# Gathers kept out of the first three retrievals, embedding products in other PSUM banks, two first-stage blocks run earlier

## The chip, the cores and the metric

The kernel runs on one core of one Trainium2 chip. The metric is the device time of one execution in microseconds (us). Five engines run side by side, each in the order of its own instruction list: TensorE (PE, matmuls; PEld is its weight loads), VectorE (DVE), ScalarE (ACT), GpSimd (POOL, which issues the indirect gathers) and SyncE (SP, which issues the other transfers).

## What is computed

One layer of a decoder for 512 prompt tokens and 64 sample tokens (576 in all), model width 1024. First comes a projection with window attention and a gated unit, and their merge. Then a layer of experts, PEER: every token scores 2 x 128 keys for each of 8 heads, takes the best 16 of the 16 x 16 pairs of a head ("retrieval"), and uses those 16 of 16384 one-neuron experts. Last comes a gated embedding.

```python
    def one_block(xb):
        q = (xb @ w_q).reshape(blk, PEER_HEADS, 2, PEER_HALF)
        sc = jnp.einsum('thcd,hcnd->thcn', q, sub_keys).astype(jnp.float32)
        s_top, i_top = lax.top_k(sc, PEER_TOPK)
        ...
        best, pos = lax.top_k(cand, PEER_TOPK)
        idx = jnp.take_along_axis(cand_idx, pos, axis=-1)
        gate = jax.nn.softmax(best, axis=-1)
        u = expert_u[idx]
        act = jax.nn.gelu(jnp.einsum('thkd,td->thk', u, xb).astype(jnp.float32))
        w = (gate * act).astype(xb.dtype)
        return jnp.einsum('thk,thkd->td', w, expert_v[idx])
...
    x2 = x1 + _peer(_rms_norm(x1, lp['ffn_norm_g']), ...)
    gate = jax.nn.sigmoid(_rms_norm(x2, lp['ple_norm_g']) @ lp['w_ple_gate'])
    x3 = x2 + gate * (p_i @ lp['w_ple'])
```

## The kernel before

Tokens lie in five tiles: the 64 sample tokens and four of 128. The experts of the first two tiles (192 tokens) are *gathered*: for every token and each of 128 slots a row of `peer_u`, and later one of `peer_v`, comes by an indirect transfer (L720, 512 KB each). A gather of `peer_u` ends in one DVE instruction that multiplies and sums (L732), one of `peer_v` in one that scales and adds (L739). That makes 192 + 192 = 384 gathers. The other three tiles (384 tokens) go through *all* experts as dense matmuls: stage 1 multiplies the tokens with each of 128 blocks of `peer_u`, GELU follows, the result is multiplied with a gate matrix G that is zero but at the retrieved experts, and stage 2 multiplies it with `peer_v`.

In float32 a product is made of three matmuls of halves: `split` writes the high half of a weight block on ACT (`w_hi`, L69) and the rest on DVE (`w_lo`, L70). The weight tiles have three or four buffers.

The program after the projections, in the order in which it is written:

- *Retrievals* `retrieve(0)` to `retrieve(2)`, nearly all DVE work: candidates (L624 to L629), the best 16 (L637 to L641), and lookups by comparison and sum (L682, L658, L660, L666, L699), with copies on ACT between (L645, L692). They are written as generators; at each of their steps one first-stage block `stage1()` is placed (24 matmuls at L85, GELU at L789, in turn into the PSUM banks `pv` and `mm`), until `S1_TOPK[ti]` blocks stand in all. At some steps a tile of the embedding product `ple()` (L828, 12 matmuls of 512 columns, emptied by ACT at L830) and of a transpose of rows (`x1_rows()`, L842) follows.
- *Gate phase*: 24 steps `tb`. `build_g` makes the one-hot operands `oa` and `ob` (L862, L865, L868 on DVE, L859 and L860 on ACT) and multiplies them on PE into the banks `sc` and `pt` (L876), which ACT empties (L882). `make_ew` (L798) turns what a retrieval found. First-stage blocks are placed until a goal per step is reached, and the last two retrievals (`retrieve(3)`, `retrieve(4)`) run in the first 7 steps.
- *Stage 2*: 128 steps `j`, each 18 matmuls (L1013), with the remaining first-stage blocks in its first 86 steps or so.

Gathers are placed by credits: `pay(x)` adds x and places as many gathers as the credit holds. `GP` is the credit per first-stage block in the three phases, `GT` the credit per step of the gate phase (its first 7 steps, and the rest), `G2` the credit per step of stage 2 (with and without a first-stage block in it). Before `retrieve(0)` is through there is nothing to gather.

A list scheduler puts the instructions of each engine in order, by the order in which they are written, by their dependencies, by raised priorities (`tc.high_priority`) and by costs of its own. Each engine then runs its list in that order.

```python
    def pay(x):
        credit[0] += x
        n = int(credit[0])
        credit[0] -= n
        gather(n, mark_pe[0])
...
        ps = (mm() if j % 2 or phase[0] > 1 else bank("pv"))[:, :NB]
```

Of the kernel before, what the change touches and what calls it, by code (L numbers as in the profile page):

```python
# [23 lines left out]
NJ = 128  # L24
TB = 16
JB = 8
GP = [0.5, 0.0, 1.65]
G2 = (1.6, 2.0)
SPILL = set(range(2, 40, 2))
NSP = len(SPILL)  # L30
GT = (2.0, 3.5)
ONE = (1, 2)
TAIL0 = 112
TAIL1 = 122
S1_TOPK = (4, 9, 13)
TBK = 7
S1_END = 6
RUN = 2
# [12 lines left out]
def tile_decoder_step(ctx: ExitStack, tc: tile.TileContext, a, o):  # L51
# [16 lines left out]
    def split(src, hi, lo):  # L68
        A.activation(hi, src, AF.Copy)  # L69
        V.tensor_sub(lo, src, hi.bitcast(F32))  # L70
# [59 lines left out]
    def bank(tag):  # L130
        return psB.tile([P, 512], F32, name=tag)
# [47 lines left out]
    with tc.high_priority(offset=500):  # L179
        for cols in HALVES:  # L180
            ps = bank("sc")[:, :cols.stop - cols.start]
# [63 lines left out]
    for g in range(4):  # L245
# [7 lines left out]
        if g == 0:  # L253
            pv = bank("pt")
# [3 lines left out]
            pv = bank("pt")  # L258
# [279 lines left out]
    for c0, r in tilesA:  # L538
# [4 lines left out]
        for hh in range(2):  # L543
            hs = slice(hh * 512, (hh + 1) * 512)
            pt = bank("pt")
# [180 lines left out]
    def gather_steps():  # L726
        for ti, ns in ((0, NS), (1, P)):
            dots = gp.tile([P, P], F32, name="dots")
            wts = gp.tile([P, P], F32, name="wts")
            for s in range(ns):  # L730
                row_ = gather_row(a["peer_u"], ixs[ti][:, s:s + 1])
                V.scalar_tensor_tensor(row_, row_, 1.0, xrs[ti], op0=ALU.mult, op1=ALU.mult,  # L732
                                       accum_out=dots[:, s:s + 1])
                yield
            A.activation(wts[:, :ns], dots[:, :ns], AF.Gelu_apprx_tanh)
            V.tensor_tensor(wts[:, :ns], wts[:, :ns], gts[ti][:, :ns], op=ALU.mult)
            for s in range(ns):
                row_ = gather_row(a["peer_v"], ixs[ti][:, s:s + 1])
                V.scalar_tensor_tensor(accs[ti], row_, wts[:, s:s + 1], accs[ti], op0=ALU.mult, op1=ALU.add)  # L739
                yield  # L740
# [22 lines left out]
# [5 lines that stand above are left out]
# [7 lines left out]
    def stage1():  # L775
        nonlocal j1, nlive
        j = j1
        j1 += 1
        w = load_block(a["peer_uT"][j])
        ps = (mm() if j % 2 or phase[0] > 1 else bank("pv"))[:, :NB]  # L780
        tform(ps, w, xb)
        if j in SPILL:
            act = held_x[-1][:, sorted(SPILL).index(j) % 6, :]
        else:
            n = nlive % RING
            nlive += 1
            act = held_x[n // 6][:, n % 6, :] if n < NXP - 6 else (
                acp[0][:, n - NXP + 6, :] if n < RING - 6 else held_x[-1][:, n - RING + 6, :])
        A.activation(act, ps, AF.Gelu_apprx_tanh)  # L789
        acts[j] = act  # L790
        if j in SPILL:
            S.dma_start(ad[sorted(SPILL).index(j)], act)
        pay(GP[phase[0]])

    def make_ew(e0, e1_, gtf):
        pt = bank("pt")
        for q, src in enumerate((e1_, gtf, e0)):
            T.transpose(out=pt[:, q * P:(q + 1) * P], in_=src, identity=ident)  # L798
        ew = ep.tile([P, 4, P], F32, name="ew")
        A.activation(ew[:, 1:4, :], pt[:, 0:3 * P].rearrange("p (a b) -> p a b", a=3), AF.Copy)  # L800
        A.activation(ew[:, 0, :], pt[:, P:2 * P], AF.Copy, scale=-1.0)
        ewT.append(ew)
# [7 lines left out]
    def ple():  # L810
        ws_ = []
        for k in range(2):
            raw = wp.tile([P, D], F32, name="w_raw", bufs=4)
            S.dma_start(raw, a["w_ple"][k])
            ws_.append([plp.tile([P, D], F32R, name=nm) for nm in ("wph", "wpl")])
            split(raw, *ws_[k])
        for c0, r in TILES:
            pt = plp.tile([P, 2, P], F32, name="pt")
            S.dma_start(pt[:, :, :r], a["pT"][:, :, c0:c0 + r])
            ph, pl = (plp.tile([P, 2, P], F32R, name=nm) for nm in ("ph", "pl"))  # L820
            split(pt[:, :, :r], ph[:, :, :r], pl[:, :, :r])
            for hh in range(2):
                st = plp.tile([P, 512], F32, name="st")
                ps = bank("pv")
                hs_ = slice(hh * 512, (hh + 1) * 512)
                for k in range(2):
                    for i, (xi, wi) in enumerate(((ph, 0), (ph, 1), (pl, 0))):
                        T.matmul(ps[:r], lhsT=xi[:, k, :r], rhs=ws_[k][wi][:, hs_],  # L828
                                 start=k == 0 and i == 0, stop=k == 1 and i == 2)
                A.activation(st[:r], ps[:r], AF.Copy)  # L830
                S.dma_start(pld[c0:c0 + r, hs_], st[:r])
            yield
# [14 lines left out]
    def build_g(tb):  # L847
# [38 lines left out]
        S.dma_start(gd[:, :, tb].rearrange("c p j t -> p c (j t)"), gs.rearrange("p (c j) t -> p c (j t)", j=JB))  # L886

    ples, xrs_ = ple(), x1_rows()
    for ti in range(3):
        for _ in retrieve(ti, ti < 2):  # L890
            if len(acts) < S1_TOPK[ti]:
                stage1()
# [3 lines left out]
        if ti == 0:  # L896
            steps.append(gather_steps())
        while len(acts) < S1_TOPK[ti]:
            stage1()
# [10 lines left out]
    for tb in range(NB // TB):  # L910
# [9 lines left out]
        if tb < TBK:  # L920
            goal = S1_TOPK[2] + (tb + 1) * (S1_PRE - S1_TOPK[2]) // TBK
        else:
# [6 lines left out]
        for _ in range(2):  # L929
            if rest_t and next(rest_t[0], 1) == 1:  # L930
                rest_t.pop(0)
                make_ew(*found[4 - len(rest_t)])
        pay(GT[tb >= TBK] if tb < 22 else 0)
    while nlive < RING - 1:
# [82 lines left out]
    for j in range(NJ):  # L1017
# [4 lines left out]
        if j and j - 1 not in SPILL and j1 < NJ:  # L1022
            stage1()
        pay(G2[0] if j1 < NJ else G2[1])
        if j == TAIL0:
# [185 lines left out]
```

## Time and profile before

| | us |
|---|---|
| median of 3 runs | 1736.32 (1732.24 to 1738.2) |
| profiled execution | 1734.34 |
| its span, first to last instruction | 1732.6 |
| first retrieval begins / first gate product / first matmul of stage 2 | 484.6 / 571.25 / 857.75 |

In the rows below, a line of the timeline gives start, duration, engine, line of the kernel, operation, output<-inputs, shapes, count, and in brackets how long the engine had stood idle before it and what ended that. Operations on DVE and matmuls on PE overlap a little at their ends, so the time that one takes is read from the start of the next. A line of stretches gives the stretch, its length, and the busy time and count for PE, PEld, DVE, ACT and POOL, then the granted PE clock (1.00 throughout), the share of DMA and GB/s.

### The profile page before, as it was taken

Reading aid. Unit: us, or ns where it says so; the run is one execution under the profiler, and the core shown is the slowest. Engines: PE = TensorE matmul, PEld = TensorE weight load, DVE = VectorE, ACT = ScalarE, POOL = GpSimd, SP = SyncE. Lnnn points to the kernel's source line nnn. Section 1 sums busy time; section 2 is a strip of 40 time slices with the busy share of each in tenths; the row PEclk is TensorE's granted clock in tenths of the full one; section 3 lists DMA queues with packets and bytes.
Section 4 is the critical chain, followed back from the end, with each engine's and each line's share of the span. In section 5 each row is a group of like instructions: output and inputs, shape, how many; then the busy total and the mean of one; then the engine's idle time right before and its main releaser. Section 6 shows DMA issues by size and latency. Waiting matters only on the chain.

```text
span 1732.6 us, 27657 instructions
## 1 busy us (share of the span) xinstructions
PE 1705.1 (98%) x10040; PEld 1554.4 (90%) x10040; DVE 1435.4 (83%) x2880; ACT 859.7 (50%) x1519; POOL 531.3 (31%) x390
## 2 busy tenths in 40 slices
PE   8999999999998999999999999999999999999998
PEld 7988999999988999999988888899988999888877
DVE  7365566579899999999698899998888988999873
ACT  6566442343366999899633333333333433333352
POOL 0000000000011122454255554555544544566400
PEclk9999999999999999999999999999999999999999
DMA  7211232432267778999899999999999999999842
GB/s 239 93 61 50 77 104 93 153 108 97 80 203 253 222 242 266 388 363 369 313 370 353 372 395 397 402 398 382 382 343 349 363 343 324 337 373 383 316 164 79
DMA packets 179481, 459.13 MB, mean 265 GB/s; under 512 B 15504, under 2 KB 78992, under 8 KB 177296
## 3 DMA queue, kind: packets, MB, share of 16 engines
q1 hardware_dynamic: 123760, 255.29, 41.8%
q0 software_dynamic: 55584, 202.07, 31.2%
q8 instruction: 79, 1.29, 0.3%
q14 instruction: 58, 0.48, 0.1%
HBM read 420.67 MB, written 37.36 MB: 264 GB/s over the span
## 4 chain that ended last, share of the span: by engine, by line
PE 77%; DVE 9%; DMA 7%; issue 4%; ACT 2%; POOL 1%; SPq 0%; DVEq 0%; POOLq 0%; ACTq 0%
PE mm L85 35%; PE oacc L1013 24%; PE pv L85 5%; PE pt L876 2%; DMA row<-peer_u,idx 2%; PE oacc L974 2%; PE sc L876 2%; DVE w_lo L70 2%; PE sc L85 1%; POOL row L720 1%; DMA row<-peer_v,idx 1%; DMA x1c<-ad 1%; PE mm L974 1%; DVE row L732 1%; DVE acc L739 1%
## 5 line engine op out<-in xcount | busy, mean ns | idle before, releaser
L69 ACT ACTIVATE w_hi<-w_raw 128x1024 fp32r<-128x1024 f32 x321 | 340.2, 1060 | 365.0 <-PE mm L85 267.4
L720 POOL DMA_INDIRECT row<-peer_u,idx x192 | 262.1, 1365 | 820.4 <-PE pv L85 467.5
L70 DVE TENSOR_TENSOR w_lo<-w_raw,w_hi 128x1024 fp32r<-128x1024 f32 x321 | 391.4, 1219 | 66.7 <-ACT w_hi L69 66.1
L85 PE MATMUL mm<-xd,w_hi 128*128 128x384 f32 x1552 | 400.1, 338 | 0.0
L720 POOL DMA_INDIRECT row<-peer_v,idx x192 | 267.8, 1395 | 237.9 <-DVE acc L739 213.8
L85 PE MATMUL mm<-x,w_hi 128*128 128x320 f32 (+1 forms) x1504 | 305.3, 297 | 0.5 <-ACT qp L749 0.5
L85 PEld LDWEIGHTS mm<-xd,w_hi 128*128 128x128 f32 x1552 | 280.3, 188 | 6.2
L85 PE MATMUL mm<-xd,w_lo 128*128 128x384 f32 x776 | 262.0, 338 | 0.0
L739 DVE SCALAR_TENSOR_TENSOR acc<-row,wts,acc 128x1024 f32<-128x1024 f32 x192 | 245.6, 1279 | 5.1 <-DMA row<-peer_v,idx 4.8
L85 PEld LDWEIGHTS mm<-x,w_hi 128*128 128x128 f32 x1504 | 239.6, 188 | 8.7 <-issue 6.5
L732 DVE SCALAR_TENSOR_TENSOR row<-row,xr 128x1024 f32<-128x1024 f32 x192 | 231.7, 1218 | 14.3 <-DMA row<-peer_u,idx 14.2
L1013 PE MATMUL oacc<-w_hi,wh 128*128 128x512 f32 x768 | 241.5, 395 | 1.2 <-ACT wh L69 1.2
L1013 PE MATMUL oacc<-w_hi,wl 128*128 128x512 f32 x768 | 241.6, 396 | 0.9 <-DVE wl L70 0.9
L1013 PE MATMUL oacc<-w_lo,wh 128*128 128x512 f32 x768 | 241.5, 396 | 0.3 <-DVE w_lo L70 0.3
L85 PE MATMUL mm<-x,w_lo 128*128 128x320 f32 (+1 forms) x752 | 221.2, 294 | 0.0
L1013 PEld LDWEIGHTS oacc<-w_hi,wl 128*128 128x128 f32 x768 | 144.2, 188 | 36.3 <-DVE wl L70 1.6
L1013 PEld LDWEIGHTS oacc<-w_lo,wh 128*128 128x128 f32 x768 | 144.3, 188 | 35.0 <-DVE w_lo L70 0.7
L1013 PEld LDWEIGHTS oacc<-w_hi,wh 128*128 128x128 f32 x768 | 143.6, 188 | 30.2 <-ACT wh L69 1.5
L85 PEld LDWEIGHTS mm<-xd,w_lo 128*128 128x128 f32 x776 | 146.2, 188 | 0.1
L85 PEld LDWEIGHTS mm<-x,w_lo 128*128 128x128 f32 x752 | 141.1, 188 | 1.0 <-issue 0.8
L85 PE MATMUL pv<-xd,w_hi 128*128 128x384 f32 x496 | 131.3, 341 | 0.0
L69 ACT ACTIVATE wh<-x 128x384 fp32r<-128x384 f32 x66 | 34.7, 526 | 164.6 <-PE oacc L1013 160.9
(332 smaller groups left out, 2311.6 us busy)
## 6 DMA issues: line engine op xcount, KB each, us to landing
w_raw<-peer_uT SPq DMA_DIRECT2D x128, 512.0 KB, 6.5
w_raw<-peer_v SPq DMA_DIRECT2D x128, 512.0 KB, 6.8
gd<-gs SPq DMA_DIRECT2D x24, 1024.0 KB, 7.9
gs<-gd SPq DMA_DIRECT2D x15, 1536.0 KB, 9.8
w_raw<-w_in SPq DMA_DIRECT2D x30, 512.0 KB, 3.4
w_raw<-peer_wq SPq DMA_DIRECT2D x16, 512.0 KB, 3.5
w_raw<-w_br SPq DMA_DIRECT2D x8, 512.0 KB, 3.2
w_raw<-w_out SPq DMA_DIRECT2D x8, 512.0 KB, 3.3
```

The costliest lines, as they stand in the source:

```text
L69: A.activation(hi, src, AF.Copy)
L70: V.tensor_sub(lo, src, hi.bitcast(F32))
L85: mark_pe[0] = T.matmul(ps, lhsT=w[wi][:, wk + k, :], rhs=x[xi][k], start=i == 0, stop=i == n - 1)
L720: ins = G.indirect_dma_start(out=row_, out_offset=None, in_=table, in_offset=bass.IndirectOffsetOnAxis(ap=ix, axis=0))
L732: V.scalar_tensor_tensor(row_, row_, 1.0, xrs[ti], op0=ALU.mult, op1=ALU.mult, accum_out=dots[:, s:s + 1])
L739: V.scalar_tensor_tensor(accs[ti], row_, wts[:, s:s + 1], accs[ti], op0=ALU.mult, op1=ALU.add)
L876: ins = T.matmul(pt[:, t * P:(t + 1) * P], lhsT=oa[:, t, :], rhs=ob[:, t, :], start=True, stop=True)
L974: T.matmul(p[:r, :hs.stop - hs.start], lhsT=xi[:, k, :r], rhs=w[k][wi][:, hs], start=k == 0 and xi is xh and wi == 0, stop=k == KC - 1 and ...
L1013: mark_pe[0] = T.matmul(oacc[t][hh], lhsT=wi[:, ts], rhs=vi[:, hh * 512:(hh + 1) * 512], start=j == 0 and last == 0 and vi is vh, stop=j = ...
```

## The change

Four numbers and one name change. No credit is paid for blocks among the retrievals, less in the first 7 steps of the gate phase, and a little more in stage 2. Ten and fifteen instead of nine and thirteen blocks stand at the end of the second and third retrieval; the goals of the gate phase stay, so its first 7 steps place 18 blocks and not 20. The embedding products go to the banks `sc` and `pt` in turn.

```diff
-GP = [0.5, 0.0, 1.65]
-G2 = (1.6, 2.0)
+GP = [0.0, 0.0, 1.65]
+G2 = (1.66, 2.06)
...
-GT = (2.0, 3.5)
+GT = (1.5, 3.5)
...
-S1_TOPK = (4, 9, 13)
+S1_TOPK = (4, 10, 15)
...
             for hh in range(2):
                 st = plp.tile([P, 512], F32, name="st")
-                ps = bank("pv")
+                ps = bank(("sc", "pt")[hh])
```

By the credits, 4 gathers stood before the gate phase and 71 before stage 2, and now 0 and 63; the last one stands in step 119 of stage 2 both times.

What the scheduler makes of it shows at three places. The first is PE at the first embedding tile (the 64 sample tokens, L828) after the fifth first-stage block. Before:

```order
L85 MATMUL pv<-xd,w_lo 128x384
L828 MATMUL pv<-wph,ph 64x512
L828 MATMUL pv<-wpl,ph 64x512
L828 MATMUL pv<-wph,pl 64x512
L828 MATMUL pv<-wph,ph 64x512
L828 MATMUL pv<-wpl,ph 64x512
L828 MATMUL pv<-wph,pl 64x512
L85 MATMUL mm<-xd,w_hi 128x384 x2
```

Now, at the same place:

```order
L85 MATMUL pv<-xd,w_lo 128x384
L828 MATMUL sc<-wph,ph 64x512
L828 MATMUL sc<-wpl,ph 64x512
L828 MATMUL sc<-wph,pl 64x512
L828 MATMUL sc<-wph,ph 64x512
L828 MATMUL sc<-wpl,ph 64x512
L828 MATMUL sc<-wph,pl 64x512
L828 MATMUL pt<-wph,ph 64x512
L828 MATMUL pt<-wpl,ph 64x512
L828 MATMUL pt<-wph,pl 64x512
L828 MATMUL pt<-wph,ph 64x512
L828 MATMUL pt<-wpl,ph 64x512
```

Before, the second half of the tile stood in the middle of the next block; now both halves stand together, in two tags of banks that no block uses.

The second place is PE at the first gate product (L876). Before, after 402 first-stage matmuls:

```order
L85 MATMUL pv<-xd,w_hi 128x384 x2
L85 MATMUL pv<-xd,w_lo 128x384
L876 MATMUL pt<-ob,oa 128x128
L876 MATMUL sc<-ob,oa 128x128 x4
L876 MATMUL pt<-ob,oa 128x128 x3
```

Now, after 430:

```order
L85 MATMUL mm<-xd,w_lo 128x384
L85 MATMUL mm<-xd,w_hi 128x384
L876 MATMUL pt<-ob,oa 128x128 x2
L876 MATMUL sc<-ob,oa 128x128 x4
L876 MATMUL pt<-ob,oa 128x128 x2
```

The first product has moved behind 28 more first-stage matmuls.

The third place is DVE ahead of the operands of that product (`ob` by L862 and L868, `oa` by L865). Before:

```order
L639 MAX best<-c_6706 128x8
L680 TENSOR_TENSOR d_6734<-ib 128x8x15
L641 MAX_INDEX pos<-best,c_6706 128x8
L732 SCALAR_TENSOR_TENSOR row,dots<-row,xr 128x1024
L638 MATCH_REPLACE c_6712<-best,cand 128x50
L862 TENSOR_TENSOR ob<-c_iota,ew 128x512
L868 TENSOR_SCALAR ob<-c_iota,ew 128x128 x2
L70 TENSOR_TENSOR w_lo<-w_raw,w_hi 128x1024
L865 TENSOR_TENSOR oa<-c_iota,ew 128x512
```

Now:

```order
L658 TENSOR_TENSOR pr<-ge,cst 128x2048
L694 TENSOR_REDUCE den<-gate 128x8
L666 TENSOR_TENSOR l_6792<-pr 128x1024
L70 TENSOR_TENSOR w_lo<-w_raw,w_hi 128x1024
L666 TENSOR_TENSOR l_6794<-l_6792 128x512
L660 TENSOR_TENSOR pr<-ge,d_6784 128x2048
L666 TENSOR_TENSOR l_6796<-l_6794 128x256
L666 TENSOR_TENSOR l_6939<-pr 128x1024
L70 TENSOR_TENSOR w_lo<-w_raw,w_hi 128x1024
L862 TENSOR_TENSOR ob<-c_iota,ew 128x512
L865 TENSOR_TENSOR oa<-c_iota,ew 128x512
L868 TENSOR_SCALAR ob<-c_iota,ew 128x128 x4
```

No gather stands there any more, and lookups of the fourth retrieval (L658, L660, L666), which stood behind the first products, now stand ahead of them.

## Prediction

> **What bounds the kernel now.** I read the page's busy times first, then busy times by stretch, then the rows of TensorE (PE) that carry a wait, then the rows of VectorE (DVE) around one point.
>
> ```profile
> PE 1705.1 (98%) x10040; PEld 1554.4 (90%) x10040; DVE 1435.4 (83%) x2880; ACT 859.7 (50%) x1519; POOL 531.3 (31%) x390
> ...
> core 0: us, PE busy (x) PEld busy (x) DVE busy (x) ACT busy (x) POOL busy (x), PEclk, DMA share, GB/s
> 490.00:570.00 80.00, 71.25 (x394) 65.67 (x393) 77.29 (x307) 49.93 (x71) 13.16 (x10) 1.00 0.76 249
> ...
> 700.00:840.00 140.00, 140.00 (x950) 136.25 (x949) 137.76 (x271) 128.65 (x308) 65.12 (x46) 1.00 1.04 369
> ...
> 1050.00:1100.00 50.00, 48.86 (x232) 41.92 (x231) 46.11 (x75) 16.81 (x23) 24.30 (x19) 1.00 1.03 413
> ...
> 1500.00:1600.00 100.00, 100.00 (x430) 80.58 (x429) 97.29 (x96) 36.70 (x48) 68.27 (x48) 1.00 0.99 371
> ```
>
> PE has work 98% of the span, and the change takes no matmul away. So it can gain only time in which PE waits, and lose by making new waits. While the first three retrievals run (490 to 570 us) PE stands idle for 80.00 - 71.25 = 8.75 us while DVE is busy 77.29 of 80 us; in the gate phase proper (700 to 840) both are full. These are the PE waits from 490 us to the end of the gate phase (a small one of 0.16 us left out):
>
> ```profile
> 501.06 0.44 PE L828 MATMUL pv<-wph,ph 128*64 128x512 f32 x1 [2.22 <-ACT x L789]
> 524.68 0.50 PE L828 MATMUL pv<-wph,ph 128*128 128x512 f32 x1 [2.80 <-ACT x L789]
> 552.32 0.50 PE L828 MATMUL pv<-wph,ph 128*128 128x512 f32 x1 [2.64 <-ACT x L789]
> 566.64 0.30 PE L798 MATMUL pt<-c_ident,e 128*128 128x128 f32 x1 [0.92 <-DVE best L639]
> 584.73 1.13 PE L876 MATMUL pt<-ob,oa 128*128 128x128 f32 x8 [0.38 <-DVE oa L865]
> 619.30 0.46 PE L876 MATMUL pt<-ob,oa 128*128 128x128 f32 x2 [0.49 <-DVE best L639]
> 631.58 0.77 PE L876 MATMUL pt<-ob,oa 128*128 128x128 f32 x4 [0.50 <-DVE best L639]
> 696.01 0.68 PE L876 MATMUL pt<-ob,oa 128*128 128x128 f32 x4 [1.22 <-DVE ob L868]
> ```
>
> The embedding products (L828) wait three times, 2.22 + 2.80 + 2.64 = 7.66 us, for ScalarE (ACT) to empty a bank `pv` that a first-stage block (L85) filled; that GELU (L789) comes late behind a table load, as at 521.52 us:
>
> ```profile
> 521.52 1.28 ACT L789 ACT_TABLE_LOAD   x1
> 522.82 0.49 ACT L789 ACTIVATE x<-mm 128x384 f32<-128x384 f32 x1
> ...
> 524.15 0.48 ACT L789 ACTIVATE x<-pv 128x384 f32<-128x384 f32 x1
> ```
>
> The other waits are for DVE, 0.92 + 0.38 + 0.49 + 0.50 + 1.22 = 3.51 us. All together it is 11.2 us, and that is the most that this part of the program can give.
>
> **The change, part by part.**
>
> *Other banks.* `sc` and `pt` are not written by first-stage blocks, so the three waits for L789 go: up to -7.66 us on PE. The new banks are emptied by ACT too (L830). But with two buffers a bank of `sc` comes up again only after two tiles, and one of `pt`, which the row transposes (L842) also use, after one, and between two tiles stand two blocks, 8.3 us by the rows below. The nearest row is the wait of 2.80 us: a bank emptied that late would still be free in time. I take 0 for new waits there and keep 0 to 7.66 as bounds (the upper end is a rival).
>
> *Two blocks moved.* A block is 24 matmuls and takes 4.16 us, by the starts of two that follow each other:
>
> ```profile
> 478.40 0.51 PE L85 MATMUL mm<-xd,w_hi 128*128 128x384 f32 x2
> ...
> 482.56 0.51 PE L85 MATMUL pv<-xd,w_hi 128*128 128x384 f32 x2
> ...
> 571.25 0.46 PE L876 MATMUL pt<-ob,oa 128*128 128x128 f32 x2
> ```
>
> The work is the same wherever it stands; what counts is when PE arrives at the first gate product (571.25 us) and whether DVE has its operands then. By the order of the instructions PE has issued 402 first-stage matmuls ahead of that product before, and 430 now: 28 more, 28/24 x 4.16 = 4.85 us. Without the L828 waits and the 0.92 PE would be there at 571.25 + 4.85 - 7.66 - 0.92 = 567.5 us. Each moved block also issues a 512 KB load on SP's queue earlier, and one of them a store of its activations; the DMA share there is 0.76, against 1.04 in the gate phase, so I cost these at 0. Behind them on SP stand the embedding's stores, which nobody reads before the tail, and the loads of the row transposes, which have a block's time to land. ACT gets two more splits, with 50 us of 80 in use.
>
> *Gathers.* The credits give 4 gathers less by the end of the retrievals (4 to 0) and 4 less in the first seven steps of the gate phase (0.5 x 7, rounded by the credits): 63 instead of 71 when stage 2 begins. Each is one DVE instruction of 1.14 us; 8 are 9.1 us off DVE ahead of stage 2. POOL issues fewer, and is not near its limit (13 of 80 us).
>
> *What DVE does instead.* This is the step that I weigh most. The rows are those of DVE from the third retrieval's comparison (L682) on, and the last operand of the first product (L865):
>
> ```profile
> 546.15 0.64 DVE L637 MAX8 best<-cand 128x8 f32<-128x50 f32 x5
> 546.71 1.21 DVE L682 TENSOR_TENSOR ge<-sp,cst 128x2048 bf16<-128x2048 bf16 x1
> 547.83 1.22 DVE L70 TENSOR_TENSOR w_lo<-w_raw,w_hi 128x1024 fp32r<-128x1024 f32 x1
> 548.97 1.22 DVE L658 TENSOR_TENSOR pr<-ge,cst 128x2048 bf16<-128x2048 bf16 x1
> 550.10 1.22 DVE L732 SCALAR_TENSOR_TENSOR row<-row,xr 128x1024 f32<-128x1024 f32 x1
> ...
> 551.24 1.22 DVE L70 TENSOR_TENSOR w_lo<-w_raw,w_hi 128x1024 fp32r<-128x1024 f32 x1
> 552.38 0.68 DVE L666 TENSOR_TENSOR l<-pr 128x1024 bf16<-128x1024 bf16 x1
> 552.98 0.28 DVE L694 TENSOR_REDUCE den<-gate 128x8 f32<-128x128 f32 x1
> ...
> 570.42 0.69 DVE L865 TENSOR_TENSOR oa<-c_iota,ew 128x512 f32<-128x512 f32 x1
> ```
>
> By the starts, a split, a comparison and a gather take 1.13 to 1.14 us each, the L666 0.60. From L682 to the end of that L865 (571.1 us) it is 24.4 us, and DVE is idle nowhere in it: it comes just in time for PE at 571.25. In the new order the stretch between the same two marks has two gathers less (-2.3) and one split more (+1.1), and the work of the *fourth and fifth* retrieval now stands in it, which stood behind the first products: three operations of 128x2048 (3 x 1.13 = 3.4), four L666 (0.60 + 0.60, and two smaller ones that I estimate at 0.5 together, by their half and quarter width), and 27 small ones. Five of these take 0.56 us here (546.15 to 546.71), so 27 take at least 3.0; others have a preloading row too, and I take 3.9. The sum is -2.3 + 1.1 + 3.4 + 1.7 + 3.9 = +7.8 us: 32.2 us.
>
> The stretch starts earlier by the three gathers ahead of it (3 x 1.14 = 3.4 us), and perhaps by a part of these waits, of which the first goes with its gather:
>
> ```profile
> 513.16 1.23 DVE L732 SCALAR_TENSOR_TENSOR row<-row,xr 128x1024 f32<-128x1024 f32 x1 [0.65 <-DMA row<-peer_u,idx]
> ...
> 530.53 1.23 DVE L699 TENSOR_TENSOR ge<-sp,cst 128x2048 bf16<-128x2048 bf16 x1 [1.36 <-ACT sp L645]
> ```
>
> So the operands of the first product come at 546.71 - 3.4 - 0.65 + 32.2 = 574.9 us, where PE wants them at 567.5. PE waits some 7.4 us there (or for the splits of the blocks shortly ahead, which comes to the same): the wait for the bank has become a wait for DVE. Against before PE is then 571.25 + 4.85 - 574.9 = 1.2 us ahead. Bounds: 2.6 ahead if the 1.36 goes as well, 1.0 behind if the small operations cost 0.2 us each (+1.5) and no DVE wait goes (+0.65).
>
> Behind the first product DVE has that much retrieval work done and four gathers less, so that PE is the slower one. Of the four waits that are left there (0.38 + 0.49 + 0.50 + 1.22 = 2.59) I take half as gone: -1.3, with bounds of -2.6 and +2.
>
> *Stage 2.* Eight gathers more, through 1.66 and 2.06 per step. DVE is at 97.29 of 100 us late in the program, in this pattern of one step:
>
> ```profile
> 1548.37 0.56 DVE L70 TENSOR_TENSOR wl<-aL,wh 128x384 fp32r<-128x384 f32 x1
> 1548.85 1.28 DVE L739 SCALAR_TENSOR_TENSOR acc<-row,wts,acc 128x1024 f32<-128x1024 f32 x1
> 1550.05 1.22 DVE L70 TENSOR_TENSOR w_lo<-w_raw,w_hi 128x1024 fp32r<-128x1024 f32 x1
> ...
> 1552.57 0.56 DVE L70 TENSOR_TENSOR wl<-x,wh 128x384 fp32r<-128x384 f32 x1
> ```
>
> A step lasts 4.20 us; DVE works 0.48 + 1.14 + 2 x 1.20 = 4.02. With 0.06 x 1.20 it is 4.09, still inside, so this costs nothing as long as one late gather (1.20 us, made good in seven steps) is covered by the two buffers of `wl`. About 1090 us, where DMA moves 413 GB/s, PE has lost time already (0.88 us in this row, and 0.26 ahead of it):
>
> ```profile
> 1092.99 0.73 PE L1013 MATMUL oacc<-w_hi,wl 128*128 128x512 f32 x2 [0.88 <-DVE wl L70]
> ```
>
> I take half of that 1.14 again, +0.6, with bounds 0 and +9.6 (all eight on the path). The sum is -1.2 - 1.3 + 0.6 = -1.9 us. The profiled execution took 1734.34 us for a span of 1732.6, 1.98 us under the median of the runs, 1736.32; so I forecast 1736.3 - 1.9 = 1734.4 us. Differences under 0.3% (5.2 us) can't be told from no change in this kernel.
>
> **The rivals.**
>
> *The gain is kept.* If DVE does serve the first product by 567.5 us, all 7.66 + 0.92 us are saved, and the end of the gate phase is set by DVE's own work, which is 9.1 us shorter: 1736.3 - 9.1 + 0.6 = 1727.8 us. For it speaks that DVE's sum up to the end of the gate phase does fall by that much; against it that its order puts 9 us of later retrievals ahead of the first product, with no idle time there to take them. It decides if the operands come more than 4 us before my 574.9. Beside it stands a rule of the Trainium skill (Perfetto Trace Analysis, Identifying the Most-Contended Engine): headroom of TensorE is read from the busy share of weight loads, not of matmuls. By it the room from 490 to 570 us would be 80 - 65.67 = 14.3 us and the two blocks (8.3) would vanish in it, with this rival's time. The trace bears it out only in part: late in stage 2 weight loads are at 80.58 of 100 us with PE never waiting. Chance 0.15.
>
> *The banks don't help.* If ACT empties `sc` and `pt` as late as it did `pv`, PE keeps its 7.66 us, arrives at 571.25 + 4.85 = 576.1 with DVE ready, and nothing is won: 1736.3 us. ACT's waits for DVE ahead of L645 speak for it, the two tiles between uses against. Chance 0.12.
>
> *Slower.* The eight gathers fall on the path of stage 2, 8 x 1.20 = 9.6 us, where gathered rows land late at 413 GB/s: 1736.3 - 2.5 + 9.6 = 1743.4 us. It decides once DVE needs over 4.20 us per step, or its rows come later than the split buffers cover; the pattern above leaves 0.11 us a step. Chance 0.10.
>
> **How the numbers follow.** My forecast has 0.63, with a range of its own of 1730.5 to 1738 (the bounds of the first product, of the later waits and of stage 2's small loss). Faster by over 0.3% is the first rival and a tail of mine, 0.15 + 0.05; slower is the last rival and a tail, 0.10 + 0.03; the rest, 0.67, is no change. The range of 8 in 10 takes in the first rival's time and half of the way to the last: 1727.5 to 1740 us.
>
> **What would show it.** Right: no PE wait at L828 for L789; a PE wait of 5 to 8 us in all for DVE from 555 to 577 us, at L876 or at splits; the first gate product at 574 to 576 us; the first matmul of stage 2 some 2 us earlier than before; DVE 98 to 99% busy from 1500 to 1600 without PE idle. Wrong: the first gate product before 571, a wait at L828 for L830, or PE idle beyond 1100 us.

## The result, and the profile after

The changed kernel took 1750.55 us (median of 6 runs, 1746.92 to 1752.18) against 1736.76 for the kernel before, run beside it: a ratio of 1.0081, 95% interval [1.0065, 1.0097]. It is slower by 14 us, outside the range given.

In the profiled executions the span grew by 15.2 us, from 1732.6 to 1747.8. The first view of the changed kernel has its mean granted clock, which was 1.000 before; the second is the page's busy times, the third the busy times by stretch (PE, PEld, DVE, ACT, POOL, PEclk, DMA share, GB/s).

```profile
core 0: 1747.8 us, clock 0.994
```

```profile
PE 1713.4 (98%) x10040; PEld 1562.9 (89%) x10040; DVE 1437.8 (82%) x2880; ACT 858.7 (49%) x1519; POOL 526.5 (30%) x390
```

```profile
490.00:570.00 80.00, 77.03 (x425) 72.73 (x424) 77.37 (x330) 53.60 (x73) 5.83 (x5) 0.98 0.68 221
...
1050.00:1100.00 50.00, 46.46 (x222) 39.66 (x220) 42.62 (x68) 16.96 (x23) 23.77 (x18) 1.00 1.00 397
1100.00:1150.00 50.00, 48.84 (x233) 43.09 (x234) 46.54 (x75) 16.36 (x22) 26.16 (x19) 0.97 0.98 376
1150.00:1200.00 50.00, 46.98 (x227) 42.07 (x226) 43.26 (x66) 15.83 (x22) 26.26 (x19) 0.97 0.98 379
1500.00:1600.00 100.00, 100.00 (x436) 81.37 (x436) 96.02 (x96) 36.61 (x48) 65.31 (x48) 1.00 0.99 368
```

From 490 to 570 us PE does 5.8 us more than before, as hoped, and late in stage 2 it is never idle. The loss lies between: from 1050 to 1200 us PE is idle for 3.54 + 1.16 + 3.02 us, and in two of the three stretches the granted clock is below 1. The rows of PE with the waits:

```profile
554.19 0.66 PE L842 MATMUL pt<-c_ident,xc 128*128 128x128 f32 x4 [1.21 <-ACT st L830]
556.18 1.09 PE L842 MATMUL pt<-c_ident,xc 128*128 128x128 f32 x4 [1.34 <-DMA xc<-x1d]
...
575.46 1.20 PE L876 MATMUL pt<-ob,oa 128*128 128x128 f32 x4 [4.87 <-DVE ob L868]
...
728.36 0.49 PE L876 MATMUL pt<-ob,oa 128*128 128x128 f32 x2 [2.54 <-DVE ob L868]
...
860.03 0.73 PE L1013 MATMUL oacc<-w_hi,wh 128*128 128x512 f32 x2 [0.63 <-ACT wh L69]
...
1085.14 0.73 PE L1013 MATMUL oacc<-w_hi,wl 128*128 128x512 f32 x2 [0.70 <-DVE wl L70]
...
1099.89 0.74 PE L1013 MATMUL oacc<-w_lo,wh 128*128 128x512 f32 x2 [2.40 <-DVE w_lo L70]
1101.80 1.22 PE L1013 MATMUL oacc<-w_hi,wl 128*128 128x512 f32 x2 [1.17 <-DVE wl L70]
1102.81 1.05 PE L1013 MATMUL oacc<-w_hi,wh 128*128 128x512 f32 x2
...
1105.27 0.62 PE L1013 MATMUL oacc<-w_hi,wh 128*128 128x512 f32 x2
...
1156.19 0.59 PE L85 MATMUL mm<-xd,w_lo 128*128 128x384 f32 x1 [3.02 <-DVE w_lo L70]
```

Two things are to be seen. First, PE waits for DVE's part of a split, `w_lo`. Secondly, behind the waits at 1099.89 and 1101.80 the same two matmuls take 1.05 us instead of 0.62 for some microseconds. Stage 2, from its first matmul (857.75 us before, 860.03 now) to its last (1670.25 and 1685.42), went from 812.5 to 825.4 us, +12.9. Of that, waits of 0.25 us and more are 8.1 us against 1.1 before (+7.0). Two stretches of half clock of 3.41 us each (from 1101.72 and from 1156.34 us) cost 2 x 3.41 / 2 = 3.4 us. And 11 first-stage matmuls were put off into stage 2 (1584 instead of 1573 stand behind its first matmul), 11 x 0.174 = 1.9 us. That is 12.3 of 12.9.

Why `w_lo` came late is seen on DVE, ahead of the wait at 1099.89:

```profile
1092.04 1.23 DVE L732 SCALAR_TENSOR_TENSOR row<-row,xr 128x1024 f32<-128x1024 f32 x1 [0.72 <-DMA row<-peer_u,idx]
...
1094.92 1.23 DVE L732 SCALAR_TENSOR_TENSOR row<-row,xr 128x1024 f32<-128x1024 f32 x1 [1.64 <-DMA row<-peer_u,idx]
...
1097.47 1.23 DVE L732 SCALAR_TENSOR_TENSOR row<-row,xr 128x1024 f32<-128x1024 f32 x1 [1.32 <-DMA row<-peer_u,idx]
...
1098.62 1.22 DVE L70 TENSOR_TENSOR w_lo<-w_raw,w_hi 128x1024 fp32r<-128x1024 f32 x1
```

Three gathers stand in DVE's list ahead of that split, and each waits for its row: DVE is idle for 3.68 us with work behind it that it may not start.

### The profile page after: what moved, and what is told of

Same layout as the page of the kernel before. It is cut to its first block, busy times and chain, and to the rows that moved or that the text cites. A ratio compares the mean times of both kernels' runs of the same rounds, so it can differ in the third digit from the quotient of the medians.

```text
span 1747.8 us, 27683 instructions
## 1 busy us (share of the span) xinstructions
PE 1713.4 (98%) x10040; PEld 1562.9 (89%) x10040; DVE 1437.8 (82%) x2880; ACT 858.7 (49%) x1519; POOL 526.5 (30%) x390
## 4 chain that ended last, share of the span: by engine, by line
PE 73%; DVE 12%; DMA 6%; issue 5%; POOL 2%; ACT 2%; SPq 0%; DVEq 0%; POOLq 0%; ACTq 0%
PE mm L85 33%; PE oacc L1013 23%; PE pv L85 4%; DVE w_lo L70 3%; PE pt L876 2%; DMA row<-peer_v,idx 2%; POOL row L720 2%; PE sc L876 2%; DMA row<-peer_u,idx 2%; PE oacc L974 2%; PE sc L85 1%; PE mm L974 1%; DMA x1c<-ad 1%; ACT w_hi L69 1%; DVE row L732 1%
## 5 line engine op out<-in xcount | busy, mean ns | idle before, releaser
L69 ACT ACTIVATE w_hi<-w_raw 128x1024 fp32r<-128x1024 f32 x321 | 340.2, 1060 | 366.7 <-PE mm L85 275.7
L720 POOL DMA_INDIRECT row<-peer_v,idx x192 | 262.8, 1369 | 233.8 <-DVE acc L739 175.2
```

Of the source, the lines that this page charges most:

```text
L720: ins = G.indirect_dma_start(out=row_, out_offset=None, in_=table, in_offset=bass.IndirectOffsetOnAxis(ap=ix, axis=0))
```

## The experiments

The theory (A in the texts): the gathers' credits alone make the loss. In stage 2 the DMA engines are full from 1000 to 1160 us, where eight loads of G are issued from 1019 to 1174 us (one in about 50 us earlier, one in 67 later), so a faster pace makes rows late, and DVE, which keeps its order, makes PE wait. The rivals: the place of the bursts and not the pace; the gathers missing ahead of stage 2; DVE's own time; the blocks or the banks. In the runs the kernel before took 1734.9 to 1736.0 us, and every ratio is to it.

### Which part of the change

*Banks alone.*

```diff
-                ps = bank("pv")
+                ps = bank(("sc", "pt")[hh])
```

> The kernel before with only the embedding products' banks changed (sc and pt for pv). Theory (the working of the prediction): the three waits of PE on L789 of together 7.66 us go, but DVE's order up to the operands of the first gate product is the same, so that PE waits there instead, 5 to 8 us near 565 to 572 us: 1736 us, within 2 us; if that wait is long enough to halve the granted clock, 1.7 us more. Rival (the 7.66 us are kept): 1728 to 1730 us.

It took 1735.61 us, ratio 0.9999 [0.9988, 1.0010]. The waits on L789 are gone, and one long wait stands in their place, earlier than I had put it, at a row transpose that needs a bank which ACT empties late:

```profile
552.93 1.11 PE L842 MATMUL pt<-c_ident,xc 128*128 128x128 f32 x4 [8.00 <-ACT st L830]
```

ACT came to that bank late, behind a copy that waits for DVE and then splits, GELUs and table loads (left out here):

```profile
544.20 1.91 ACT L645 ACTIVATE sp<-pos 128x2048 bf16<-128x2048 uint32 x1 [3.10 <-DVE pos L641]
...
552.27 0.60 ACT L830 ACTIVATE st<-pt 128x512 f32<-128x512 f32 x1
```

8.00 us for the 7.66: nothing is won, and the rival of this run (the 7.66 us are kept) is refuted. But the time came out as expected for another reason than the one given. PE did not wait for DVE at the first gate product (570.87 us, no wait). ACT emptied the new banks as late as it had emptied `pv` (552.17 us in the kernel before), which is the mechanism of the prediction's second rival, *The banks don't help*.

*Banks and blocks, with all credits of before.*

```diff
+                ps = bank(("sc", "pt")[hh])
...
-S1_TOPK = (4, 9, 13)
+S1_TOPK = (4, 10, 15)
```

> The changed kernel with all gather credits of before (GP, G2 and GT as before); only the banks and the two blocks are moved. Theory A: stage 2 is that of before (812 to 815 us, waits under 2 us), and the gate phase has PE waits of about 5 us at the first gate product: 1735 to 1739 us. Rival C or a rival by which the blocks and banks themselves spoil stage 2: 1744 to 1751 us, with PE waits on w_lo between 1085 and 1160 us as in the changed kernel.

1734.97 us, ratio 0.9991 [0.9980, 1.0001]. Stage 2 takes 812.1 us, as before. So neither part makes the loss. Ahead of the first gate product, where PE waits 1.31 us for DVE, the long wait is now one for a load of the row transposes:

```profile
562.45 1.09 PE L842 MATMUL pt<-c_ident,xc 128*128 128x128 f32 x4 [7.25 <-DMA xc<-x1d]
```

*Credits alone.*

```diff
-GP = [0.5, 0.0, 1.65]
-G2 = (1.6, 2.0)
-GT = (2.0, 3.5)
+GP = [0.0, 0.0, 1.65]
+G2 = (1.66, 2.06)
+GT = (1.5, 3.5)
```

> The kernel before with only the gather credits changed (GP, GT and G2); banks and blocks as before. Theory A: stage 2 is that of the changed kernel (waits on w_lo of 2 to 3 us near 1100 and 1156 us, 9 to 12 us longer than before), and ahead of it at most 3 us are lost: 1744 to 1751 us. Rival (the changed kernel's loss needs the blocks or banks too, since they shift the first-stage blocks against the gathers): 1736 to 1740 us.

1749.85 us, ratio 1.0085 [1.0069, 1.0101]: the whole loss, with stage 2 at 823.5 us and the waits at the place expected (1.90 and 1.17 us on `w_lo` and `wl` at 1102 to 1104 us, 0.60 and 1.16 at 1086 to 1088, and a clock of 0.93 from 1100 to 1150), though none at 1156.

*The pace of stage 2, taken out of the change and put into the kernel before.*

> The changed kernel with G2 put back from (1.66, 2.06) to (1.6, 2.0); banks, blocks and the gate phase's credits stay as changed. By the credits 362 instead of 370 gathers are then done at j = 112 and 2 are left for j = 122. Theory A (stage 2 lost 10.5 us because 0.06 more gathers per step, on DMA engines already full around 1090 us, make DVE wait for rows ahead of w_lo): the waits of PE of 2.40 and 3.02 us on w_lo are gone, the waits in stage 2 sum to under 2.5 us, the time is 1738 to 1741 us (the 2.3 us lost before stage 2 stay). Rival B (the total does not matter, only where the fractions of the credits put a burst of gathers against the splits): some waits of 2 to 3 us stay at other places, 1743 to 1751 us. Rival C (the loss comes from the 9 gathers that are missing before stage 2, which must be caught up at whatever pace): as B in time, with the waits at 1090 to 1160 us still there.

1741.02 us, ratio 1.0027 [1.0015, 1.0040]. The waits on `w_lo` and `wl` in stage 2 sum to 2.05 us, the clock stays at 1.00 there, and 9.5 of the 13.8 us are gone. Stage 2 still takes 816.0 us, 3.5 more than before: 1.9 are the 11 first-stage matmuls put off into it, about 1 is longer waits. The pace is not all.

> The kernel before with only G2 raised from (1.6, 2.0) to (1.66, 2.06). Theory A: the DMA engines at their limit around 1090 us get 0.06 more gathers per step, DVE waits longer for rows, PE waits 2 us or more at one or two places and the granted clock falls there: 1742 to 1748 us. Rival B (it is the place of the bursts): anything from 1735 to 1748 us, with waits at other places than in the changed kernel. Rival C (the gathers missing before stage 2): no change, 1736 us within 2 us, since 71 gathers are done ahead of stage 2 as before.

1742.77 us, ratio 1.0038 [1.0025, 1.0051], the time that A had and against rival C, since here, by the credits, 71 gathers are done ahead of stage 2 as before. These are its waits there; the places are nearly those of the changed kernel. The longest is as long as A had it, but the clock did not fall behind it:

```profile
1085.76 0.73 PE L1013 MATMUL oacc<-w_hi,wl 128*128 128x512 f32 x2 [1.24 <-DVE wl L70]
...
1099.05 0.74 PE L1013 MATMUL oacc<-w_lo,wh 128*128 128x512 f32 x2 [0.66 <-DVE w_lo L70]
1100.66 0.73 PE L1013 MATMUL oacc<-w_hi,wl 128*128 128x512 f32 x2 [0.88 <-DVE wl L70]
...
1152.82 0.45 PE L85 MATMUL mm<-xd,w_lo 128*128 128x384 f32 x1 [2.27 <-DVE w_lo L70]
```

*Twice the step of the pace*, G2 = (1.72, 2.12) in the kernel before.

> The kernel before with G2 raised twice as far, to (1.72, 2.12). With G2 at (1.66, 2.06) it took 1742.8 us against 1736.0. Theory A (the pace against a full DMA): the waits on w_lo between 1085 and 1160 us grow and more places have them, with the half clock behind: 1747 to 1758 us. Rival B (the place of the bursts, not the pace): no order between dose and time, 1735 to 1745 us as likely as more.

1744.16 us, ratio 1.0053 [1.0038, 1.0067], under what A had. The interval overlaps that of the single step, so an order between dose and time is not shown, and this run does not decide against B. It has six waits of 0.4 us and more, the longest 1.17 us, spread from 991 to 1101 us, and no low clock behind any of them. Against B stands that stage 2 takes 819.5 to 825.4 us in all four kernels with a raised pace and all of G's bytes (821.3 in this one), and at most 816.1 us in those with the old pace. How the lateness of the rows is cut into waits may set a part of the price; that is not shown.

### Full DMA engines, or a full DVE

The changed kernel, with half of the bytes of each load of G:

```diff
-                S.dma_start(gsl[:, :nb], gd[j // JB][:, :nb])
+                S.dma_start(gsl[:, :12], gd[j // JB][:, :12])
...
-        V.tensor_tensor(wfv, wfv, gsl[:, :, j % JB, :], op=ALU.mult)
+        V.tensor_tensor(wfv, wfv, gsl[:, None, :12, j % JB, :].to_broadcast([P, 2, 12, TB]), op=ALU.mult)
```

> The changed kernel with half of the bytes of every load of G in stage 2 left out (12 of 24 blocks of gd are loaded and multiplied twice, so the other half of G is not used); DVE's instructions, their order from the first steps of stage 2 on, and all gathers stay. Theory A (rows come late because the 16 DMA engines are full between 1000 and 1160 us, where G is loaded every 26 us): 0.79 MB less per load takes about 30 GB/s of 397 off there, the rows are on time, PE's waits of 2.40 and 3.02 us on w_lo and the half clock behind them go, stage 2 is 812 to 816 us, the time 1738 to 1742 us. Rival D (DVE itself is full there, 46 to 49 of 50 us, and the gathers' own DVE time is what delays w_lo): the two waits stay above 2 us, 1747 to 1752 us.

1735.91 us, ratio 1.0005 [0.9997, 1.0014], even better than A had it. Stage 2 takes 812.9 us, as A had it; the rest may be chance ahead of it, since in the profile it begins at 856.8 us, and at 860.0 and 861.3 us in two others whose order is the same up to its first steps (the changed kernel, and it with the old pace). The first view is what DVE waited for from 1060 to 1165 us in the kernel before (us in all, times, longest), the second the same in the changed kernel, the third with half of G's bytes, the fourth the busy times with half of G's bytes:

```profile
DVE row L732 <- DMA row<-peer_u,idx: 4.8, 7, 1.3
```

```profile
DVE row L732 <- DMA row<-peer_u,idx: 9.5, 10, 2.3
```

```profile
DVE row L732 <- DMA row<-peer_u,idx: 1.0, 3, 0.6
```

```profile
1050.00:1100.00 50.00, 50.00 (x241) 43.54 (x240) 48.60 (x80) 17.74 (x25) 26.31 (x20) 1.00 1.01 386
1100.00:1150.00 50.00, 50.00 (x247) 44.36 (x246) 49.84 (x80) 17.90 (x25) 30.33 (x21) 1.00 1.00 379
```

DVE is busier than in the slow kernel, 48.60 and 49.84 of 50 us, and PE has no idle time at all. So D is refuted: DVE's own time was not the limit, the rows' lateness was. It settles the cause in stage 2: all gathers are there, at the new pace, and the loss is gone with the bytes that competed with them.

### The gate phase's part

Without the new pace the change still lost 4.7 us by the ratio. In the following rows of that kernel (G2 old) PE has made the transposes of what the third retrieval found (L798) by 567.4 us; ACT copies them at 570.96, behind splits and GELUs, and PE gets its first gate product at 575.92:

```profile
567.14 0.27 PE L798 MATMUL pt<-c_ident,e 128*128 128x128 f32 x1
...
570.96 0.49 ACT L800 ACTIVATE ew<-pt 128x384 f32<-128x384 f32 x1
...
575.92 1.19 PE L876 MATMUL pt<-ob,oa 128*128 128x128 f32 x4 [4.68 <-DVE ob L868]
```

So there I moved these transposes and copies ahead in the order:

```diff
         if tb == 0:
-            make_ew(*found[2])
+            with tc.high_priority(offset=1500):
+                make_ew(*found[2])
```

> The changed kernel with the old pace G2 (the one at 1741.0 us), and the transposes and copies that make the first gate operands (make_ew of the third retrieval) put ahead in the order, on ACT and PE; nothing else. Theory (PE's wait of 4.7 us ahead of the first gate product comes from these copies, which ACT does 4 us after PE's transposes, and from the fourth retrieval's steps that DVE then has ahead of the operands): the wait falls under 1.5 us and the half clock behind it goes: 1734.5 to 1737 us. Rival (DVE sets the pace of the whole stretch, so that the wait only moves to another place of the gate phase): 1739.5 to 1742 us.

1733.48 us, ratio 0.9985 [0.9976, 0.9994]: 7.5 us less than without it, and 0.15% faster than the kernel before. The copy now stands at 567.00 and the wait is 0.55 us:

```profile
561.48 0.48 PE L798 MATMUL pt<-c_ident,e 128*128 128x128 f32 x1 [0.96 <-ACT st L844]
...
567.00 0.47 ACT L800 ACTIVATE ew<-pt 128x384 f32<-128x384 f32 x1
...
572.33 1.13 PE L876 MATMUL pt<-ob,oa 128*128 128x128 f32 x8 [0.55 <-DVE oa L865]
```

The wait of 2.85 us at 729.11 us is gone as well, and in the profiles stage 2 begins at 853.9 instead of 861.3 us (single executions, which differ by 4.5 us in this with the same order). So it was the order in the lists that cost here. This kernel still has the eight gathers missing ahead of stage 2, and the old pace there, and it loses nothing: the raised pace was not needed to make them good.

> The same reordering on the kernel with banks and blocks changed and all old credits (1735.0 us; its waits there are 7.25 us at the x1 transposes and 1.31 us at the first product). Theory: the 1.31 us go, the 7.25 us, which a load of xc sets, stay: 1732.5 to 1735 us. Rival (DVE is full from 490 to 660 us, 76.8 of 80 and 89.7 of 90 us): no change, 1734.5 to 1736.5 us.

1734.21 us, ratio 0.9998 [0.9989, 1.0008]. With the old credits the same reordering gives nothing that can be measured; PE's wait for the load of `xc` at 561.83 us stays, 7.24 us.

> As the one before, with the gathers of the first-stage blocks put off (GP 0 instead of 0.5, as in the change) but made good inside the gate phase (GT (2.0, 3.8) instead of (2.0, 3.5)), so that by the credits 71 gathers are done before stage 2, as in the kernel before; G2 old. Theory (putting gathers off is harmless as long as stage 2 does not have to make them good): stage 2 takes 812 to 814 us, and the gate phase gains: 1729 to 1734 us. Rival (the DMA engines are 0.98 to 1.00 busy in 660 to 860 us too, so rows come late there at 3.8 a step, and DVE keeps gate operands waiting behind them): PE waits over 2.5 us near 700 to 760 us with half clock, 1736 to 1741 us.

1734.59 us, ratio 0.9995 [0.9986, 1.0004], between theory and rival. PE waits 2.84 us for ACT at the first gate product (572.31 us), and twice later in the gate phase for DVE, under 2 us each:

```profile
728.23 0.68 PE L876 MATMUL pt<-ob,oa 128*128 128x128 f32 x4 [1.76 <-DVE ob L868]
...
747.20 0.68 PE L876 MATMUL pt<-ob,oa 128*128 128x128 f32 x4 [1.89 <-DVE ob L868]
```

Stage 2 has no wait of 0.3 us or more and takes 808.5 us. So putting gathers off is harmless where it is made good ahead of stage 2, though it does not gain there either.

*Two more blocks*, S1_TOPK = (4, 10, 17), on banks and blocks with the old credits.

> The kernel with banks and blocks changed and the old credits (the one at 1735.0 us), with two more first-stage blocks moved ahead of the gate phase, S1_TOPK (4, 10, 17). Theory (PE idles 7.25 and 1.31 us ahead of and at the first gate product because DVE is late with its operands, and a moved block fills 4.16 us of this): 8.3 us more of work stand there, the waits shrink to about 2 us, the clock stays full: 1727 to 1731 us. Rival (DVE is full there, 76.8 of 80 and 89.7 of 90 us, so each block's 1.14 us split and what is shifted in the gate phase pushes the operands back, and PE then waits in the gate phase): 1733 to 1737 us.

1734.99 us, ratio 1.0000 [0.9991, 1.0009]; the rival was right. PE has 75.55 instead of 72.17 us of work from 490 to 570, and 84.12 instead of 87.78 from 570 to 660. Waits of 1.94 and 1.77 us appear at the added blocks' splits and one of 4.41 at a gate product. DVE sets the pace of this stretch.

### The price of a long wait

> The kernel before, with the subtraction that makes wl (0.47 us each in a row) done 8, 2, 4, 6, 8 and 12 times more at j = 92, 95, 98, 101, 104 and 107, so that DVE, which has 4.02 to 4.09 of 4.20 us a step there, is late by known amounts. The first 8 should be mostly taken up by what is prepared ahead; the others make waits of PE of about 1, 2, 3, 4 and 5.5 us. Theory H (an idle of PE of 2.4 us or more halves the granted clock for some 3.5 us, one under 2 us does not): full clock behind the short ones, half clock behind the waits of 3 us and more, each costing 1.5 to 2 us beyond the wait: 1752 to 1760 us. Rival (the half clock in the changed kernel had another cause): clock 1.00 throughout stage 2, and the time is longer by the waits alone.

```diff
         split(wf, wh, wl)
+        for _ in range({92: 8, 95: 2, 98: 4, 101: 6, 104: 8, 107: 12}.get(j, 0)):
+            V.tensor_sub(wl, wf, wh.bitcast(F32))
```

1780.45 us, ratio 1.0266 [1.0247, 1.0284], more than expected. The scheduler set gathers of 1.20 us between the added subtractions, so that the doses came out as five waits, all of them long:

```profile
1528.97 2.93 PE L1013 MATMUL oacc<-w_hi,wl 128*128 128x512 f32 x6 [7.78 <-DVE wl L1057]
...
1561.50 2.93 PE L1013 MATMUL oacc<-w_hi,wl 128*128 128x512 f32 x6 [4.61 <-DVE wl L1057]
...
1581.27 2.93 PE L1013 MATMUL oacc<-w_hi,wl 128*128 128x512 f32 x6 [5.45 <-DVE wl L1057]
...
1602.57 2.93 PE L1013 MATMUL oacc<-w_hi,wl 128*128 128x512 f32 x6 [6.64 <-DVE wl L1057]
...
1625.87 2.93 PE L1013 MATMUL oacc<-w_hi,wl 128*128 128x512 f32 x6 [9.01 <-DVE wl L1057]
```

The waits sum to 33.5 us, the span grew by 1775.7 - 1732.6 = 43.1. The difference, 9.6 us, is 1.9 us for each wait: behind every one of them the first seven to eleven matmuls take 0.43 us each (the first of all 0.59) instead of 0.233. It is the half clock alone: PE was busy for 19.25 us at half clock there, and half of that is 9.6 us. H holds for waits of 4.6 us and more; the short doses, which were to tell the threshold, did not come about, and the last section takes it from the other traces.

## Why the prediction was wrong

- *Banks: right in the time, only in part in the mechanism.* The waits on L789 went and the time did not move (banks alone 0.9999). In the changed kernel the first gate product came at 575.46 us, forecast for 574.9, after a wait of 4.87 us for DVE (forecast some 7.4, partly at splits). The rest are new waits ahead of it that I had taken as 0: 0.42 us (at L828 for L830, named as a sign of a wrong forecast) and 1.21 us for banks that ACT emptied late, and 1.34 us for a load of `xc`. With the banks alone ACT's lateness was all of the wait (8.00 us), and with banks and blocks the load was most of it (7.25 us). That nothing would be won held each time; that DVE would be the reason held in the whole change alone, and for the banks alone it was luck.
- *The two blocks and the banks together: right in the time.* Their own part is 0.9991 [0.9980, 1.0001] against the forecast of -1.9 us for the whole. The first rival (the gain is kept) fell with the same runs, and with it, in this stretch, the rule of the Trainium skill (Perfetto Trace Analysis, Identifying the Most-Contended Engine) that stood beside it: two further blocks moved into the room that weight loads leave gave 1.0000, with new waits at their splits.
- *Behind the first product: wrong.* I had PE 1.2 us ahead there and a further 1.3 us saved in later waits. Instead 1.9 us of first-stage work were put off into stage 2, which began 2.3 us later in the profile (less than the 4.5 us by which single executions differ in this), and with the old pace 4.7 us were lost in all. Two things were missed. The clock fell: from 576 to 580 us PE issued 21 matmuls at a mean clock of 0.56, where the kernel before issued 31 at 1.00. And later waits did not shrink: one of 2.54 us stood at 728.36 instead of the one of 1.22 at 696.01, for gate operands that DVE had behind late rows.
- *Stage 2: wrong, and this decides.* The term was +0.6 us with bounds of 0 and 9.6; it measured 12.9, of which 1.9 is work put off. The step that failed is "so this costs nothing" and the half of 1.14 us taken beside it. The first was worked out from a step at 1550 us, where it held (PE 100.00 of 100 us). But the pace rises from 1000 to 1160 us as well, where DMA was at 413 GB/s and a share of 1.03 in the kernel before and PE had already lost 1.14 us; half the bytes of G removed the loss (1.0005). The rival "slower" named this mechanism and place. I gave it 0.10 and bounded its price by DVE's own time, 8 x 1.20 us. That was the wrong measure: by these runs the price is how long DVE stands still behind a missing row (9.5 us of DVE in that stretch, against 4.8 before), plus the clock.
- *The chance.* A resource with a share of 1.03 and a wait already behind it, to which the change adds load, should have had the larger chance.

## What to carry to other kernels

Where an engine works in the order of its list, an operation that waits for a transfer holds up everything behind it; before raising the pace of such operations, look for the stretch where the DMA share is 1 and a wait for them already shows, not at the mean or at the quiet pattern. Cost a wait of TensorE of 4 us or more at its length plus some 2 us (1.6 to 2.5 us here). And when removing work does not speed up the operation that is waited for, look at what stands between its producers in the other engines' lists: here three transposes and two copies, moved ahead by a priority, were worth 7.5 us in one kernel, and nothing in another whose long wait was for a load.

## What was not expected of the hardware

The granted clock of PE halves behind long waits. These are the stretches around the first gate product of the changed kernel (PE busy, PEld, DVE, ACT, POOL, PEclk, DMA share, GB/s):

```profile
572.00:576.00 4.00, 0.54 (x2) 0.57 (x3) 4.00 (x9) 3.19 (x10) 0.00 (x0) 0.58 0.70 236
576.00:580.00 4.00, 4.00 (x21) 4.00 (x20) 3.04 (x7) 1.02 (x2) 0.94 (x1) 0.56 0.21 64
580.00:584.00 4.00, 4.00 (x31) 4.00 (x30) 3.33 (x6) 4.00 (x11) 0.00 (x0) 1.00 0.62 202
```

The length of a wait does not decide alone: the clock fell behind 1.89 us (747.20, late gate credits), and it did not behind 2.22, 2.80 and 2.64 us in the kernel before. What does decide shows when time is cut into windows of 3.41 us. Every stretch of half clock between 480 us and the end of stage 2 lasts 3.41 us, or two or three times that, and those of one execution begin whole multiples of 3.41 us apart, so they lie on a fixed grid. In the 14 traces of this study, from 480 us to the end of stage 2, the clock went from full to half behind each window of that grid in which PE was busy for 1.54 us or less, and behind none in which it was busy for 1.56 us or more. In the following rows each window stands with the next one. The first pair is at the wait of 1.89 us, the second and third are the nearest to the limit on its two sides (kernel before with the new pace):

```profile
745.24:748.65 3.41, 1.52 (x14) 1.48 (x14) 3.41 (x8) 0.62 (x2) 0.62 (x1) 1.00 1.05 413
748.65:752.07 3.42, 3.42 (x15) 3.42 (x14) 2.89 (x8) 2.63 (x5) 1.15 (x1) 0.50 1.06 394
...
522.92:526.33 3.41, 1.54 (x8) 0.94 (x7) 3.41 (x7) 3.40 (x5) 0.47 (x1) 1.00 1.04 403
526.33:529.74 3.41, 3.41 (x12) 2.83 (x11) 3.41 (x7) 0.64 (x3) 1.41 (x1) 0.50 1.06 400
...
1150.97:1154.38 3.41, 1.56 (x9) 1.56 (x10) 3.22 (x6) 1.06 (x1) 1.68 (x1) 1.00 1.03 408
1154.38:1157.79 3.41, 3.41 (x20) 3.23 (x19) 3.41 (x5) 1.02 (x2) 1.01 (x1) 1.00 1.03 411
```

And this is the wait of 2.80 us in the kernel before. The grid, laid there from its only half-clock stretch after 480 us, at 1731.70 us, cuts the wait in two, and neither window has enough of it:

```profile
519.96:523.38 3.42, 1.93 (x10) 1.31 (x8) 3.13 (x6) 3.38 (x6) 0.00 (x0) 1.00 1.01 369
523.38:526.79 3.41, 2.11 (x11) 1.79 (x12) 3.41 (x6) 2.27 (x4) 1.88 (x1) 1.00 1.04 394
```

So neighbouring waits add up within a window (2.40 and 1.17 us about 1100 us in the changed kernel). An estimate from the limit: 3.41 - 1.54 = 1.87 us of idle time in one window are enough, so that a wait from about 1.9 to 3.7 us may go either way, by where the grid cuts it, and a longer one brings the clock down in any case. The Trainium skill (TensorE: Matmul & The Clock Gate, Part 1) states that the clock goes to half after an idle window of about 3.4 us and back after as long a busy one, and that the window runs freely and does not start anew with a kernel. The traces agree as to the half, the length of the window and its fixed grid. They differ as to the idle window: one in which PE was busy for up to 1.54 us was enough.
